# Loading b in 2 MB pairs on SyncE's queue, in a batched 64x64 matmul

## The chip, the cores and the metric

One NeuronCore of one Trainium2 chip runs the whole kernel. The metric is device time in microseconds (us), the median of several executions. The profile is that of one further execution, and its times count from the start of its span.

## The reference

1024 independent products of 64x64 matrices, in fp32:

```python
def setup_inputs():
    return {
        "a": np.random.randn(1024, 64, 64).astype(np.float32),
        "b": np.random.randn(1024, 64, 64).astype(np.float32),
    }

def reference(a, b):
    return np.matmul(a, b).astype(np.float32)
```

Each of `a`, `b` and the output is 16.8 MB in memory, so 33.55 MB are read and 16.78 MB written.

## The kernel before, in words

The batch is cut in 16 tiles `t` of 64 matrices for `b` and the output (1 MB each), and in 8 steps `s` of 128 matrices for `a` (2 MB each); step `s` serves tiles `2s` and `2s+1`.

**a.** `load_a(s)` (L70) brings a step in as four quarters. Three go through GpSimd's queue, which casts them to bf16 on the way (`a_sb`, L74); the fourth goes as fp32 on SyncE's queue (`a_raw`, L78). There are three buffers of each (`A_AHEAD = 3`). Step 0 is special: `load_first_a` brings its four quarters as fp32, two on SyncE's queue and two on ScalarE's (L91). `a` has to be transposed. For steps 1 to 3 (`ON_DVE`) VectorE does that, in `transpose_dve` (L128); its fourth quarter is first cast by ScalarE (L126) out of `a_raw`. For the others `regroup` on VectorE (L109 for the three quarters, L112 for `a_raw`) is followed by transposes on TensorE (L138) and copies out on ScalarE (L141).

**The work of a tile.** `spread(t)` copies the transposed `a` into a block-diagonal tile `at_bd` on VectorE (L154 for tiles 2 to 7, L164 for the others). `cast(t)` makes bf16 out of the fp32 `b_sb` (L173, on VectorE, for tile 0 on ScalarE; the last tile in four parts on both, L178 and L180). `multiply(t)` runs 64 matmuls (L218) and copies the result out of PSUM in eight pieces, mostly on ScalarE (L206). `store(t)` writes a tile out (L195): tiles 0 to 13 on GpSimd's queue, the last two on SyncE's and ScalarE's. Stores are held back by one iteration (`HOLD = 2`).

**b.** `load_b(t)` (L94) loads one tile, 1 MB, in one transfer: even tiles are issued by SyncE, odd ones by ScalarE. `b_pool` has three buffers of 8 KB per partition. So the load of tile `t+3` can be issued when `cast(t)` has read its buffer.

**Queues.** The profile names the three queues by which transfers reach the 16 DMA engines: q0 is GpSimd's (three quarters of `a` from step 1 on, the stores of tiles 0 to 13), q1 is SyncE's (even `b` tiles, `a_raw`), q10 is ScalarE's (odd `b` tiles). Each engine issues its own transfers in program order, among its other instructions.

**Order.** The program is written out by hand (`manual_schedule`). Before the loop: the first `a`, `b` tiles 0 and 1, `load_a(1)`, `load_b(2)`, `load_a(2)`. Iteration `t` of the loop then does `spread(t+1)`, `cast(t+1)`, `load_b(t+3)`, on some even `t` a `load_a`, then `multiply(t)`, the transposing of a later step of `a`, and `store(t-1)`. On SyncE's queue the order is therefore, after the first two quarters of `a`: b0, a_raw 1, b2, a_raw 2, a_raw 3, a_raw 4, b4, a_raw 5, b6, a_raw 6, b8, a_raw 7, b10, b12, b14, stores.

Of the kernel before, what the change touches and what calls it, by code (L numbers as in the profile page):

```python
# [8 lines left out]
fp32 = mybir.dt.float32  # L9
# [4 lines left out]
def kernel(  # L14
# [14 lines left out]
    nc = tc.nc  # L29
# [3 lines left out]

    n_t, n_s = B // 64, B // 128
    A_AHEAD = 3
    B_AHEAD = 3
    N_BD = 2
    HOLD = 2
    ON_DVE = (1, 2, 3)

    a_v = a.rearrange("(s g h) (mp v) k -> s h g mp (v k)", h=4, g=32, v=16)
    b_v = b.rearrange("(t g h) (kp u) n -> t (h kp) g (u n)", h=4, g=16, u=2)
    o_v = out.rearrange("(t gh x) (mo w) n -> t (x mo) gh (w n)", gh=8, x=8, w=4)

    consts = ctx.enter_context(tc.tile_pool(name="consts", bufs=1))
    a_pool = ctx.enter_context(tc.tile_pool(name="a_pool", bufs=A_AHEAD))
    b_pool = ctx.enter_context(tc.tile_pool(name="b_pool", bufs=B_AHEAD))
    work = ctx.enter_context(tc.tile_pool(name="work", bufs=2))
    o_pool = ctx.enter_context(tc.tile_pool(name="o_pool", bufs=8))
    t_psum = ctx.enter_context(  # L50
# [11 lines left out]
    a_tiles, b_tiles, abf_tiles, at_tiles, bbf_tiles = {}, {}, {}, {}, {}  # L62
# [7 lines left out]
    def load_a(s):  # L70

        a_sb = a_pool.tile([128, 3, 16, 64], bf16, name="a_sb")
        for h in range(3):
            nc.gpsimd.dma_start(  # L74
                out=a_sb[:, h, :, :].rearrange("p v k -> p (v k)"), in_=a_v[s, h], single_packet=True
            )
        a_raw = a_pool.tile([128, 16, 64], fp32, name="a_raw")
        nc.sync.dma_start(out=a_raw[:].rearrange("p v k -> p (v k)"), in_=a_v[s, 3])  # L78
        a_tiles[s] = a_sb, a_raw

    def load_first_a():

        raw = [
            o_pool.tile([128, 8, 2, 2, 64], fp32, name="o_sb")[:].rearrange(
                "p gh j wl n -> p (gh j wl n)"
            )
            for _ in range(2)
        ]
        parts = [raw[h % 2][:, 1024 * (h // 2) : 1024 * (h // 2) + 1024] for h in range(4)]
        for h in range(4):  # L90
            (nc.scalar if h % 2 else nc.sync).dma_start(out=parts[h], in_=a_v[0, h])  # L91
        a_tiles[0] = parts

    def load_b(t):  # L94
        b_sb = b_pool.tile([128, 16, 128], fp32, name="b_sb")
        queue = nc.scalar if t % 2 else nc.sync
        queue.dma_start(out=b_sb[:], in_=b_v[t])  # L97
        b_tiles[t] = b_sb

    def regroup(s):  # L100
        a_sb = a_tiles.pop(s)
        a_bf = work.tile([128, 16, 4, 64], bf16, name="a_bf")
        if s == 0:
            for h in range(4):
                copy = nc.scalar.copy if h % 2 else nc.vector.tensor_copy
                copy(a_bf[:, :, h, :], a_sb[h].rearrange("p (v k) -> p v k", v=16))  # L106
        else:
            cast_sb, raw = a_sb
            nc.vector.tensor_copy(  # L109
                a_bf[:, :, 0:3, :], cast_sb[:].rearrange("p h v k -> p v h k")  # L110
            )
            nc.vector.tensor_copy(a_bf[:, :, 3, :], raw[:])  # L112
        abf_tiles[s] = a_bf
        at_tiles[s] = work.tile([128, 32, 4, 4, 4], fp32, name="at_sb")

    def transpose_dve(s, half):
        cast_sb, raw = a_tiles[s]
        if half == 0:
            at_tiles[s] = work.tile([128, 4, 8, 4, 4, 4], fp32, name="at_sb")
        for h in (2 * half, 2 * half + 1):  # L120
            rows = cast_sb[:, h, :, :] if h < 3 else None
            if h == 3:
                rows = work.tile([128, 16, 4, 64], bf16, name="a_bf")[:, 0:4, :, :].rearrange(
                    "p x y k -> p (x y) k"
                )
                nc.scalar.copy(rows, raw[:])  # L126
            pairs = rows.rearrange("p v k -> p (v k)").bitcast(fp32)
            nc.vector.transpose(  # L128
                at_tiles[s][:, h].rearrange("p g w mp vo -> p w vo g mp"),
                pairs.rearrange("p (vo w kp) -> p w vo kp", vo=4, w=4),  # L130
            )

    def transpose(s, j):
        a_cols = abf_tiles[s][:].rearrange("p v h k -> p v (h k)").bitcast(fp32)
        for wl in range(2):
            at_ps = t_psum.tile([128, 4, 128], fp32, name="at_ps")
            for vo in range(4):
                nc.tensor.transpose(  # L138
                    at_ps[:, vo, :], a_cols[:, 4 * vo + 2 * j + wl, :], identity[:]
                )  # L140
            nc.scalar.copy(  # L141
                at_tiles[s][:, :, 2 * j + wl, :, :],
                at_ps[:].rearrange("p vo (g mp) -> p g mp vo", mp=4),
            )

    def spread(t):
        bd = bd_tiles[t % N_BD]
        at_sb = at_tiles[t // 2]
        for h in range(4):
            rows = slice(32 * h, 32 * h + 32)  # L150
            if t // 2 in ON_DVE:
                for i in range(2):
                    block = 32 * (2 * (t % 2) + i)
                    nc.vector.tensor_copy(  # L154
                        bd[rows, 8 * i : 8 * i + 8, :, h, :, :].rearrange(
                            "p g w mp vo -> p (g w) (mp vo)"
                        ),
                        at_sb[block : block + 32, h].rearrange(
                            "p g w mp vo -> p (g w) (mp vo)"
                        ),  # L160
                    )
            else:
                half = slice(16 * (t % 2), 16 * (t % 2) + 16)
                nc.vector.tensor_copy(  # L164
                    bd[rows, :, :, h, :, :].rearrange("p g w mp vo -> p (g w) (mp vo)"),
                    at_sb[rows, half].rearrange("p g w mp vo -> p (g w) (mp vo)"),
                )

    def cast(t):
        b_bf = work.tile([128, 16, 128], bf16, name="b_bf")  # L170
        b_sb = b_tiles.pop(t)
        if t < n_t - 1:
            (nc.vector.tensor_copy if t else nc.scalar.copy)(b_bf[:], b_sb[:])  # L173
        else:
            for gq in range(4):
                rows = slice(4 * gq, 4 * gq + 4)
                if gq % 2:
                    nc.vector.tensor_copy(b_bf[:, rows, :], b_sb[:, rows, :])  # L178
                else:
                    nc.scalar.copy(b_bf[:, rows, :], b_sb[:, rows, :])  # L180
        bbf_tiles[t] = b_bf

    def store(t):
        for piece in held.pop(t):
            piece()
# [53 lines left out]
    with tc.manual_schedule():  # L239
        load_first_a()  # L240

        nc.vector.memset(warm[:, 0:1], 0.0)
        nc.scalar.copy(warm[:, 1:2], warm[:, 0:1])
        load_b(0)
        load_b(1)
        nc.vector.memset(bd_tiles[0][:], 0.0)  # L246
        make_identity(nc, identity)
        nc.gpsimd.memset(bd_tiles[1][:, 0:8], 0.0)
        load_a(1)
        load_b(2)  # L250
        nc.gpsimd.memset(bd_tiles[1][:, 8:16], 0.0)
        load_a(2)
        regroup(0)
        transpose(0, 0)
        transpose(0, 1)
        spread(0)
        cast(0)
        for t in range(n_t):
            s, half = t // 2, t % 2
            if t + 1 < n_t:  # L260
                spread(t + 1)
                cast(t + 1)
            if t + B_AHEAD < n_t:
                load_b(t + B_AHEAD)
            if half == 0 and 0 < s < n_s - 1 - A_AHEAD:
                load_a(s + 1 + A_AHEAD)
            if half == 0 and 0 < s < n_s - 1 and s + 1 not in ON_DVE:
                transpose(s + 1, 1)
            multiply(t)
            if t == 0:  # L270
                transpose_dve(1, 0)
                transpose_dve(1, 1)
                a_tiles.pop(1)
                load_a(A_AHEAD)
                load_a(A_AHEAD + 1)
            if t and s + 2 in ON_DVE and (half or s):
                for part in [0, 1] if t == 1 else [half]:
                    transpose_dve(s + 2, part)
                if half:
                    a_tiles.pop(s + 2)  # L280
            elif half == 0 and 0 < s and s + 2 < n_s:
                regroup(s + 2)
            elif half == 1 and s + 2 < n_s:
                transpose(s + 2, 0)
            if t >= HOLD - 1:
                store(t - HOLD + 1)
        for t in range(n_t - HOLD + 1, n_t):
            store(t)
# [30 lines left out]
```

## Time and profile before

| | us |
|---|---|
| median of three runs | 133.72 (133.57 to 133.80) |
| the profiled execution | 133.61 |
| its span | 131.8 |
| VectorE busy | 101.8 (77% of the span) |
| ScalarE busy | 88.1 (67%) |
| TensorE busy, matmul | 59.6 (45%) |
| GpSimd busy | 31.9 (24%) |
| one `cast` of a b tile on VectorE (L173) | 1.227 |
| from issue to landing of a 1 MB b load, median | 16.5 (14.7 to 22.0) |
| from issue to landing of a 1 MB store on GpSimd's queue, median | 22.7 |
| from issue to landing of an `a_raw` quarter (512 KB), median | 17.3 |

The span is what the instructions of the profiled execution cover; the 1.8 us between it and the time of that execution lie around it. A queue's "share of 16 engines" is the time that its packets took, divided by 16 times the span; as packets overlap a little on an engine, the shares of the queues can sum to slightly over 100%. In a timeline, the bracket behind a line tells how long the engine was idle before it, and what ended that.

### The profile page before, as it was taken

To read this page: it belongs to the slowest core of one execution; us is meant where nothing else is said; L and a number is where in the kernel's file an instruction comes from. 1 tells how busy PE (TensorE), PEld (TensorE's weight loads), DVE (VectorE), ACT (ScalarE), POOL (GpSimd) and SP (SyncE) were. 2 spreads that over 40 slices of the span, in tenths; PEclk is the share of its full clock that TensorE was granted. 3 is DMA by queue.
4 is the path that set the end of the run, shared out by engine and by line. 5 is a ranking of instruction groups with operands and counts; after the bars stand their busy time and mean duration, and the time that the engine had idled before them with its cause. 6 is when DMAs were issued, how large, how long until landed. Compare 5 with 4: busy or idle time off the path is not lost.

```text
span 131.8 us, 2750 instructions
## 1 busy us (share of the span) xinstructions
PE 59.6 (45%) x1104; PEld 56.7 (43%) x1104; DVE 101.8 (77%) x144; ACT 88.1 (67%) x158; POOL 31.9 (24%) x43
## 2 busy tenths in 40 slices
PE   0006405730550640908662883299369619465000
PEld 0006305730550630908552872298368618464000
DVE  5930399529999984999999998699999997898300
ACT  2125414999495096492999989469969996549920
POOL 8991000340054000618031204300420302040000
PEclk9999975798568555595999599558968975579855
DMA  3999999999999999999999999999999999999993
GB/s 68 372 334 313 306 313 280 280 311 321 327 299 400 362 306 297 393 393 400 321 285 357 403 395 362 308 299 385 395 391 393 390 390 397 399 395 406 390 383 136
DMA packets 19020, 44.99 MB, mean 341 GB/s; under 512 B 1088, under 2 KB 3136, under 8 KB 19008
## 3 DMA queue, kind: packets, MB, share of 16 engines
q0 software_dynamic: 6832, 20.19, 50.6%
q1 hardware_dynamic: 7120, 14.68, 30.7%
q10 hardware_dynamic: 5056, 9.96, 20.1%
q8 instruction: 8, 0.13, 0.4%
q14 instruction: 4, 0.03, 0.1%
HBM read 33.55 MB, written 16.78 MB: 382 GB/s over the span
## 4 chain that ended last, share of the span: by engine, by line
DMA 53%; ACT 15%; DVE 14%; PE 6%; issue 5%; SPq 2%; ACTq 0%; DVEq 0%
DMA b_sb<-in_b_dram 53%; ACT o_sb L206 12%; PE o_ps L218 6%; DVE at_bd L164 4%; DVE b_bf L173 4%; DVE at_bd L154 2%; ACT b_bf L173 1%; DVE at_sb L128 1%; DVE o_sb L206 1%; DVE a_bf L109 1%; SPq L91 1%; ACT a_bf L126 1%; SPq L97 1%; ACT b_bf L180 1%; DVE a_bf L112 0%
## 5 line engine op out<-in xcount | busy, mean ns | idle before, releaser
L206 ACT COPY o_sb<-o_ps 64x512 f32<-64x512 f32 x112 | 65.0, 581 | 17.9 <-PE o_ps L218 13.5
L218 PEld LDWEIGHTS <-at_bd 128*128 128x128 bf16 x1024 | 45.2, 117 | 52.6 <-DVE b_bf L173 40.5
L218 PE MATMUL o_ps<-b_bf,at_bd 128*128 128x64 bf16 x960 | 45.6, 223 | 48.7 <-DVE b_bf L173 35.0
L164 DVE COPY at_bd<-at_sb 32x1024 f32<-32x1024 f32 x40 | 29.6, 739 | 6.6 <-ACT at_sb L141 5.6
L195 POOL DMA_DIRECT2D out_dram<-o_sb x14 | 15.4, 1103 | 46.1 <-ACT at_sb L141 20.6
L154 DVE COPY at_bd<-at_sb 32x512 f32<-32x512 f32 x48 | 22.0, 457 | 1.1
L74 POOL DMA_DIRECT2D a_sb<-in_a_dram x21 | 12.4, 606 | 38.5 <-DVE at_sb L128 33.2
L173 DVE CAST b_bf<-b_sb 128x2048 bf16<-128x2048 f32 x14 | 17.2, 1227 | 5.2 <-DMA b_sb<-in_b_dram 4.9
L138 PE MATMUL at_ps<-identity,a_bf 128*128 128x128 f32 x80 | 12.9, 329 | 11.0 <-ACT a_bf L106 11.0
L138 PEld LDWEIGHTS at_ps<-identity,a_bf 128*128 128x128 f32 x80 | 11.7, 176 | 11.0 <-issue 11.0
L141 ACT COPY at_sb<-at_ps 128x512 f32<-128x512 f32 x20 | 10.8, 591 | 2.7 <-PE at_ps L138 2.0
L128 DVE STREAM_TRANSPOSE at_sb<-a_sb 128x512 f32<-128x512 f32 x9 | 8.9, 1065 | 0.0
L128 DVE STREAM_TRANSPOSE at_sb<-a_bf 128x512 f32<-128x512 f32 x3 | 3.1, 1049 | 4.0 <-ACT a_bf L126 4.0
L206 DVE COPY o_sb<-o_ps 64x512 f32<-64x512 f32 x8 | 5.5, 690 | 0.2
L106 ACT CAST a_bf<-o_sb 128x1024 bf16<-128x1024 f32 x2 | 2.1, 1045 | 5.0 <-DMA o_sb<-in_a_dram 5.0
L173 ACT CAST b_bf<-b_sb 128x2048 bf16<-128x2048 f32 x1 | 1.9, 1897 | 4.0 <-DMA b_sb<-in_b_dram 4.0
L126 ACT CAST a_bf<-a_raw 128x1024 bf16<-128x1024 f32 x3 | 3.1, 1046 | 1.7 <-DMA a_raw<-in_a_dram 1.7
L109 DVE COPY a_bf<-a_sb 128x3072 bf16<-128x3072 bf16 x4 | 4.2, 1045 | 0.0
L106 DVE CAST a_bf<-o_sb 128x1024 bf16<-128x1024 f32 x2 | 2.8, 1383 | 1.8 <-DMA o_sb<-in_a_dram 1.8
L246 DVE MEMSET at_bd<- 128x4096 f32 x1 | 3.5, 3472 | 0.8 <-issue 0.8
L206 DVE COPY o_sb<-at_ps 64x256 f32<-64x256 f32 x8 | 3.4, 422 | 0.5 <-PE at_ps L218 0.4
L180 ACT CAST b_bf<-b_sb 128x512 bf16<-128x512 f32 x2 | 1.1, 616 | 3.5 <-DMA b_sb<-in_b_dram 3.5
(16 smaller groups left out, 15.4 us busy)
## 6 DMA issues: line engine op xcount, KB each, us to landing
out_dram<-o_sb POOLq DMA_DIRECT2D x14, 1024.0 KB, 22.7
a_sb<-in_a_dram POOLq DMA_DIRECT2D x21, 256.0 KB, 15.9
a_raw<-in_a_dram SPq DMA_DIRECT2D x7, 512.0 KB, 17.3
o_sb<-in_a_dram SPq DMA_DIRECT2D x2, 512.0 KB, 5.9
o_sb<-in_a_dram ACTq DMA_DIRECT2D x2, 512.0 KB, 7.0
out_dram<-o_sb SPq DMA_DIRECT2D x2, 512.0 KB, 5.5
out_dram<-o_sb SPq DMA_DIRECT2D x2, 256.0 KB, 5.2
out_dram<-o_sb ACTq DMA_DIRECT2D x2, 256.0 KB, 4.7
```

The costliest lines, as they stand in the source:

```text
L74: nc.gpsimd.dma_start(out=a_sb[:, h, :, :].rearrange("p v k -> p (v k)"), in_=a_v[s, h], single_packet=True)
L106: copy(a_bf[:, :, h, :], a_sb[h].rearrange("p (v k) -> p v k", v=16))
L109: nc.vector.tensor_copy(a_bf[:, :, 0:3, :], cast_sb[:].rearrange("p h v k -> p v h k"))
L128: nc.vector.transpose(at_tiles[s][:, h].rearrange("p g w mp vo -> p w vo g mp"), pairs.rearrange("p (vo w kp) -> p w vo kp", vo=4, w=4),)
L138: nc.tensor.transpose(at_ps[:, vo, :], a_cols[:, 4 * vo + 2 * j + wl, :], identity[:])
L141: nc.scalar.copy(at_tiles[s][:, :, 2 * j + wl, :, :], at_ps[:].rearrange("p vo (g mp) -> p g mp vo", mp=4),)
L154: nc.vector.tensor_copy(bd[rows, 8 * i : 8 * i + 8, :, h, :, :].rearrange("p g w mp vo -> p (g w) (mp vo)"), at_sb[block : block + 32, h]. ...
L164: nc.vector.tensor_copy(bd[rows, :, :, h, :, :].rearrange("p g w mp vo -> p (g w) (mp vo)"), at_sb[rows, half].rearrange("p g w mp vo -> p ...
L173: (nc.vector.tensor_copy if t else nc.scalar.copy)(b_bf[:], b_sb[:])
L195: store_queue(t, lo).dma_start(out=o_v[t, :, lo : lo + n, :], in_=o_sb[:, lo : lo + n].rearrange("p gh j wl n -> p (gh j wl n)"),)
L206: copies[2 * par + wl](dst, src)
L218: nc.tensor.matmul(o_ps[:, gl, g % 2, j, :], at_bd[:, j, g, :, u], b_bf[:, g, 64 * u : 64 * u + 64], start=(u == 0), stop=(u == 1),)
```

## The change: b tiles 4 to 13 in pairs

Tiles of `b` are now handled as pairs, pair `p` being tiles `2p` and `2p+1`, in two buffers of 16 KB per partition. Pairs 2 to 6 are loaded by one transfer of 2 MB each, issued by SyncE. Pairs 0, 1 and 7 (`B_ALONE`) are still two transfers of 1 MB, all on SyncE's queue but tile 1. The loads of a pair are issued in the even iterations: pair `s+2` in iteration `t = 2s`, after `cast(t+1)`, which is the last reader of the buffer's former pair `s`. Ahead of the loop, tile 3 is now loaded right behind tile 2, before `load_a(2)`. SyncE's order becomes b0, a_raw 1, b2, b3, a_raw 2, pair 2, a_raw 3, a_raw 4, pair 3, a_raw 5, pair 4, a_raw 6, pair 5, a_raw 7, pair 6, b14, b15, stores. ScalarE issues b1 alone.

```diff
-    B_AHEAD = 3
+    B_ALONE = (0, 1, n_t // 2 - 1)
...
+    b_v2 = b.rearrange("(t g h) (kp u) n -> t (h kp) g (u n)", h=4, g=32, u=2)
...
-    b_pool = ctx.enter_context(tc.tile_pool(name="b_pool", bufs=B_AHEAD))
+    b_pool = ctx.enter_context(tc.tile_pool(name="b_pool", bufs=2))
...
-    def load_b(t):
-        b_sb = b_pool.tile([128, 16, 128], fp32, name="b_sb")
-        queue = nc.scalar if t % 2 else nc.sync
-        queue.dma_start(out=b_sb[:], in_=b_v[t])
-        b_tiles[t] = b_sb
+    def load_b(pair):
+        b_sb = b_pool.tile([128, 2, 16, 128], fp32, name="b_sb")
+        if pair in B_ALONE:
+            for i in range(2):
+                queue = nc.scalar if pair == 0 and i else nc.sync
+                queue.dma_start(out=b_sb[:, i], in_=b_v[2 * pair + i])
+        else:
+            nc.sync.dma_start(out=b_sb[:].rearrange("p i g n -> p (i g) n"), in_=b_v2[pair])
+        for i in range(2):
+            b_tiles[2 * pair + i] = b_sb[:, i]
...
-            (nc.vector.tensor_copy if t else nc.scalar.copy)(b_bf[:], b_sb[:])
+            (nc.vector.tensor_copy if t else nc.scalar.copy)(b_bf[:], b_sb)
...
         load_b(0)
-        load_b(1)
...
         load_a(1)
-        load_b(2)
+        load_b(1)
...
-            if t + B_AHEAD < n_t:
-                load_b(t + B_AHEAD)
+            if half == 0 and s + 2 < n_s:
+                load_b(s + 2)
```

## The prediction, made before the changed kernel ran

> **What bounds the kernel now.** I read the page's slices and queue shares first, then the queues in a short window, then the timelines of VectorE and ScalarE for who waits for a load.
>
> ```profile
> span 131.8 us, 2750 instructions
> DMA  3999999999999999999999999999999999999993
> q0 software_dynamic: 6832, 20.19, 50.6%
> q1 hardware_dynamic: 7120, 14.68, 30.7%
> q10 hardware_dynamic: 5056, 9.96, 20.1%
> ```
>
> The DMA row is full from the first slice to the last, and the shares sum to 101.4%: the 16 DMA engines are the bound, from end to end. The change moves the same bytes. So time can be gained only in the two slices that aren't full (hardly over 0.5 us), but lost wherever DMA comes to stand idle. Next, the queues in 52 to 60 us (packets, MB, share), then in 117.3 to 121 us, when only stores are left:
>
> ```profile
> q0 software_dynamic: 480, 1.70, 58.6%
> q1 hardware_dynamic: 485, 1.00, 33.1%
> q10 hardware_dynamic: 169, 0.35, 11.8%
> ```
>
> ```profile
> q0 software_dynamic: 383, 1.48, 101.9%
> ```
>
> Queues that have work take turns packet by packet (480 against 485); SyncE's and ScalarE's queues each have a turn of their own. Last, the casts on VectorE that wait for a b tile, with the end of VectorE's work, and the one cast of `a_raw` on ScalarE that waits:
>
> ```profile
> 51.23 1.23 DVE L173 CAST b_bf<-b_sb 128x2048 bf16<-128x2048 f32 x1 [2.04 <-DMA b_sb<-in_b_dram]
> ...
> 83.66 1.23 DVE L173 CAST b_bf<-b_sb 128x2048 bf16<-128x2048 f32 x1 [1.63 <-DMA b_sb<-in_b_dram]
> ...
> 112.50 1.23 DVE L173 CAST b_bf<-b_sb 128x2048 bf16<-128x2048 f32 x1 [1.19 <-DMA b_sb<-in_b_dram]
> ...
> 115.19 3.09 DVE L164 COPY at_bd<-at_sb 32x1024 f32<-32x1024 f32 x4
> ```
>
> ```profile
> 35.36 1.05 ACT L126 CAST a_bf<-a_raw 128x1024 bf16<-128x1024 f32 x1 [1.70 <-DMA a_raw<-in_a_dram]
> ```
>
> VectorE waits only 4.9 us for b in all, and is otherwise nearly without a gap: b arrives just in time, and a later b is paid at once.
>
> **Prices.** All are worked out from these rows. A store is 1.05 MB at 403 GB/s: 2.6 us of all 16 engines. A b tile: q10 moves 9.96 MB in 20.1% of 131.8 us, 2.66 us per MB, so 2.8 us; a pair 5.6, an `a_raw` (0.52 MB) 1.4. A quarter of `a` on q0: its 66.7 us less 14 stores, over 21 quarters, 1.4. In packets, by the trace's records: b tile 512 (2 KB each), store 256, `a` quarter and `a_raw` 128 each. One b packet with one q0 packet takes 0.0055 + 0.0102 = 0.0157 us. So against a full q0 a pair on one queue takes 1024 x 0.0157 = **16.0 us**; on two queues, as before, 512 rounds of 0.0212 = **10.8 us**. VectorE needs some 11.7 us for a pair (two casts, 2.46; two spreads, 6.2 to 8; copies or transposes).
>
> **The parts that cost little.** Sixteen b issues become eleven; ScalarE loses seven, with 0.02 us of its own time each and one wait of 0.8 us: 0 to 1 us off an engine 67% busy, hidden behind the casts it waits for; taken as 0. If ScalarE set the end, it would be worth at most that 1 us. No row shows the issue of a 2 MB load: bounded by that of a 1 MB load (0.71 us) and twice that, so up to 0.7 us, five times 3.5 us if nothing covered it; the queue ahead holds 5 us and more of older work each time, so 0. Behind a pair SyncE has only the next `a_raw` and the next pair, and before the change already stood 2 to 11 us on the `a_raw` issues behind a b load (L78) without anyone waiting but the cast shown. The buffers cost nothing: pair s+2 may start after cast(2s+1), exactly when its first tile could before, its second a tile sooner.
>
> The Trainium skill, "DMA: Bandwidth & Descriptors", section "Issuing engines are not separate DMA queues", says that transfers started by several engines interleave on the same 16 DMA engines, and that several issuers save only issuing time. By it the move off ScalarE's queue would cost nothing, and the sum would be 0. The rows above speak for a difference in share; I follow the rows.
>
> **The ledger: order and share on one queue.** Times before are read off the timelines. I take the pure turn-taking and let each wait delay VectorE.
>
> 1. At 22 us a_raw 1 has landed. Before, b2, a_raw 2 followed (32.0, 35.3) with b3 beside them. Now b2, b3, a_raw 2 stand in one line: 1152 packets. Left on q0: seven quarter loads of a and store 0 (issued 28.1), also some 1152. 8 + 8 + 2.7: a_raw 2 at **40.7**, 5.4 later. ScalarE's cast (1.05) ends at 41.8, the last transpose of step 2 (before 37.21 to 38.25) at 42.8: VectorE is 4.6 late. cast(3) runs 47.2 to 48.5.
> 2. Pair 2 starts at 40.7. Against it q0 has three quarter loads of a and stores 1 and 2, 896 packets: 5.6 + 9.1 + a short gap, lands about 55.4. cast(4) would be ready at 53.7 (before 49.2 + 4.5, after which it waited 2.04): it starts at 55.4, **+4.2**.
> 3. a_raw 3 and 4 follow while q0 waits for new work: 56.8 and 58.2. The transposes of step 3 end at 58.9 (before 54.35). All after is 4.5 late; cast(6) is ready at 69.7.
> 4. Pair 3 starts at 58.2; q0 has six quarter loads and stores 3 and 4, 1280 packets, so it is full: 16.0, lands **74.2**. cast(6): before 65.16, now **+9.0**. cast(7) at 79.4.
> 5. a_raw 5 (2.7), pair 4 from 76.9. Now stores come late too, since they wait for tiles: 384 packets at once, 256 at 82.4. 5.6 + 6.5: **89.0**. cast(8) ready at 85.3, starts at 89.0, **+12.8**.
> 6. q0 has run dry. Pair 5, 91.7 to about 100; cast(10) ready at 100.6 (8 + 8 less the wait of 1.63 it had at tile 9): **+11.1**. From here VectorE sets the pace, and DMA idles; cast(14) had waited 1.19, no more: spread(15) ends at 128.2, before 118.28: **+9.9**.
> 7. The tail before: 118.28 to 131.82, the last store 4.6 us behind its issue into full queues. The nearest row for an empty queue is the run's first load, 512 KB in 4.3 us, 1.4 of them moving bytes; 256 KB would so take 3.6. I take 1.0 off (bounds 0 and 2.9, the part of the 4.3 that isn't moving bytes).
>
> Sum: 131.8 + 9.9 - 1.0 = 140.7 of span; + 1.8 around it + 0.1 (the profiled run, 133.61, is 0.11 below the median) = 142.6. Against it: before, transfers on SyncE's queue landed 1 to 2.5 us sooner than pure turn-taking over the real issue times gives, those on q0 3 us later. With each pair 2 us sooner, cast(6) is +7, cast(8) +10.7, and the end 140.5. I take the middle, **141.5 us**.
>
> **Rivals.**
>
> A, *the packets grow*. If a 2 MB load is cut into 4 KB packets, SyncE's queue gets as many bytes a turn as both queues had, and a pair takes 5.6 + 5.2 = 10.8 again. Then pair 2 lands at 51.5 before its cast is ready (53.7, +2.5); pair 3, behind two `a_raw` of 1.4 to 2.7, at 65 to 67.7, before or just as its cast is ready (67.7); the old waits of 1.63 and 1.19 go, and -0.3 is left: DMA stays full, **133.7 us** (133.0 to 135.2), not slower. For it: `a_raw` and the GpSimd stores do go in 4 KB packets. Against it: b's do not, though a partition's 8 KB lies together in SBUF. It decides if the pairs show 512 packets in place of 1024. The chance is 0.13, split nearly evenly over the three outcomes.
>
> B, *q0 runs dry sooner*. Stores and `a` loads wait for the tiles that are late, so SyncE's queue gets the engines alone earlier. If pairs 3 and 4 meet q0 half empty (640 packets each, 12.1 us), pair 3 lands at 70.3, cast(6) is +5.1; pair 4 at about 83.5, after cast(8) is ready (81.4): +7.3; less 1.63 and 1.19 and the tail's 1.0: 3.5, **137.2 us** (135 to 138.5). For it: a_raw 5 to 7 had buffers to spare. Against: in step 4 q0 gets its 1280 packets by 65.5, the times of before plus 4.5, and so in time to be served against pair 3. Chance 0.12.
>
> C, *a 2 MB load leaves gaps*. If its descriptors aren't ready in time, the five pairs lose up to the 3.5 us of issue above, and as much again in the line behind them: 141.5 + 7.0, **148.5 us**, 0.03. For it speaks only that no row shows such a load; against it, that no 1 MB load leaves a gap in the DMA row.
>
> **How the numbers follow.** The forecast, with its own range 138.5 to 146, has 0.72; A 0.13, B 0.12, C 0.03. The predicted time is the forecast's. The range 135 to 146 takes in B and leaves out most of A and C, under 2 in 10; its upper end is the ledger of pure turns with no lead, no saving in the tail and 2 us for issuing. About 0.2% is what a measurement here can tell from no change. Faster: 0.06, most of it from A (and ScalarE's 1 us); same 0.04, from A; slower 0.90.
>
> **What would show it.** In the changed profile: no ScalarE queue traffic in the middle; equal packet counts of q0 and q1 wherever both have work; 1024 packets for a pair; from issue to landing about 16 us and more for the pairs; the ScalarE cast at L126 waiting some 7 us for a_raw 2; VectorE waiting for b at tiles 6 and 8 by 3 to 5 us each; stores landing much sooner than 22.7 us; and digits under 9 in the DMA row in the last third. Wrong would be: a DMA row still full to the end (then A), waits at tiles 4, 6 and 8 under 2 us each (B), or a stretch in which q1 has a pair outstanding and yet DMA isn't busy (C).

## The result, and the profile after

The changed kernel takes **141.57 us** (140.06 to 142.03, four runs) against 133.73 us (133.57 to 133.80): a ratio of 1.057, 95% interval 1.049 to 1.065. Slower, as forecast (141.5 us). The profiled execution is the shortest of its four runs: 140.06 us, with a span of 138.3. So the spans differ by 6.5 us, the medians by 7.8. One run of e9 and one of e11 below fell in a slower state, some 2% above the fastest of their kernel, and the times and ratios leave them out.

Lines of the page after; behind each queue stand packets, MB and the share of 16 engines:

```profile
span 138.3 us, 2729 instructions
DMA  3999999999999999999999999999999999995995
q0 software_dynamic: 6832, 20.19, 48.5%
q1 hardware_dynamic: 10736, 22.02, 46.8%
q10 hardware_dynamic: 1360, 2.62, 5.0%
HBM read 33.55 MB, written 16.78 MB: 364 GB/s over the span
out_dram<-o_sb POOLq DMA_DIRECT2D x14, 1024.0 KB, 11.4
```

The bytes are the same, and the DMA row is still full until the last four slices. A store on GpSimd's queue lands 11.4 us after its issue instead of 22.7: q0 is served sooner. And the engines need longer for the same `b`, fp32 `a` and last stores: q1 and q10 together have 51.8% of 138.3 us, 71.6 us, where before they had 50.8% of 131.8, 67.0 us. That is 4.7 us of the 6.5; q0's own time rose by 0.4 (48.5% of 138.3 against 50.6% of 131.8), and the rest is DMA that stands idle in the last slices (from 124 to 128 us its share is 0.57).

VectorE's and ScalarE's waits for loads, from their timelines (start, length, in brackets the idle time before):

```profile
54.97 1.23 DVE L179 CAST b_bf<-b_sb 128x2048 bf16<-128x2048 f32 x1 [2.41 <-DMA b_sb<-in_b_dram]
...
69.69 1.23 DVE L179 CAST b_bf<-b_sb 128x2048 bf16<-128x2048 f32 x1
...
85.97 1.23 DVE L179 CAST b_bf<-b_sb 128x2048 bf16<-128x2048 f32 x1 [5.46 <-DMA b_sb<-in_b_dram]
...
99.78 1.23 DVE L179 CAST b_bf<-b_sb 128x2048 bf16<-128x2048 f32 x1 [2.30 <-DMA b_sb<-in_b_dram]
```

```profile
40.46 1.04 ACT L132 CAST a_bf<-a_raw 128x1024 bf16<-128x1024 f32 x1 [6.85 <-DMA a_raw<-in_a_dram]
```

These are the casts of tiles 4, 6, 8 and 10, and the cast of a_raw 2. Last, the queues of the changed kernel from 58.8 to 62.2 us, when pair 3 is on its way:

```profile
q1 hardware_dynamic: 480, 0.98, 104.7%
q14 instruction: 1, 0.01, 0.8%
```

q0 isn't in the list: it has nothing to do, though GpSimd issued three loads from 57.49 on:

```profile
57.49 1.65 POOL L75 DMA_DIRECT2D a_sb<-in_a_dram  x3 [9.69 <-DVE at_sb L134]
```

Their first packet starts at 62.40. And q1, alone, fills all 16 engines with 0.98 MB in 3.4 us, some 290 GB/s. A full DMA row can hide a loss: here the engines are busy and slow.

### The profile page after: what moved, and what is told of

Read it like the earlier page. It is cut to its first block, busy times and chain, and to the rows that moved or that the text cites. A ratio compares the mean times of both kernels' runs of the same rounds, so it can differ in the third digit from the quotient of the medians.

```text
span 138.3 us, 2729 instructions
## 1 busy us (share of the span) xinstructions
PE 60.8 (44%) x1104; PEld 57.6 (42%) x1104; DVE 100.6 (73%) x144; ACT 87.8 (64%) x151; POOL 33.0 (24%) x43
## 3 DMA queue, kind: packets, MB, share of 16 engines
q0 software_dynamic: 6832, 20.19, 48.5%
## 4 chain that ended last, share of the span: by engine, by line
DMA 47%; SPq 22%; DVE 15%; ACT 6%; issue 4%; PE 3%; DVEq 0%; ACTq 0%
DMA b_sb<-in_b_dram 28%; DMA a_raw<-in_a_dram 19%; SPq L79 10%; SPq L100 10%; DVE at_bd L170 5%; ACT o_sb L212 5%; DVE b_bf L179 4%; PE o_ps L224 3%; DVE at_bd L160 2%; DVE o_sb L212 2%; SPq L102 1%; SPq L92 1%; DVE at_sb L134 1%; ACT a_bf L132 1%; DVE a_bf L115 1%
## 5 line engine op out<-in xcount | busy, mean ns | idle before, releaser
L224 PE MATMUL o_ps<-b_bf,at_bd 128*128 128x64 bf16 x960 | 47.7, 227 | 57.2 <-DVE b_bf L179 46.5
L224 PEld LDWEIGHTS <-at_bd 128*128 128x128 bf16 x1024 | 47.2, 120 | 61.4 <-DVE b_bf L179 49.6
L201 POOL DMA_DIRECT2D out_dram<-o_sb x14 | 16.8, 1196 | 59.0 <-ACT o_sb L212 27.0
L179 DVE CAST b_bf<-b_sb 128x2048 bf16<-128x2048 f32 x14 | 17.2, 1227 | 10.7 <-DMA b_sb<-in_b_dram 10.3
L160 DVE COPY at_bd<-at_sb 32x512 f32<-32x512 f32 x48 | 20.8, 433 | 1.1
L144 PE MATMUL at_ps<-identity,a_bf 128*128 128x128 f32 x80 | 11.8, 311 | 10.8 <-ACT a_bf L112 10.8
L144 PEld LDWEIGHTS at_ps<-identity,a_bf 128*128 128x128 f32 x80 | 10.7, 164 | 10.8 <-issue 10.8
L118 DVE CAST a_bf<-a_raw 128x1024 bf16<-128x1024 f32 x4 | 3.1, 776 | 0.0
## 6 DMA issues: line engine op xcount, KB each, us to landing
out_dram<-o_sb POOLq DMA_DIRECT2D x14, 1024.0 KB, 11.4
```

Of the source, the lines that this page charges most:

```text
L144: nc.tensor.transpose(at_ps[:, vo, :], a_cols[:, 4 * vo + 2 * j + wl, :], identity[:])
L160: nc.vector.tensor_copy(bd[rows, 8 * i : 8 * i + 8, :, h, :, :].rearrange("p g w mp vo -> p (g w) (mp vo)"), at_sb[block : block + 32, h]. ...
L201: store_queue(t, lo).dma_start(out=o_v[t, :, lo : lo + n, :], in_=o_sb[:, lo : lo + n].rearrange("p gh j wl n -> p (gh j wl n)"),)
L224: nc.tensor.matmul(o_ps[:, gl, g % 2, j, :], at_bd[:, j, g, :, u], b_bf[:, g, 64 * u : 64 * u + 64], start=(u == 0), stop=(u == 1),)
```

## The experiments

Three theories stood against each other. **Theory 1**, turns: the engines serve queues packet by packet, so b on one queue has one turn in two against GpSimd's queue, where two queues had two in three. **Theory 2**, pairing: the 2 MB transfer or the buffers that come free in pairs. **Theory 3**, order: `a_raw` stands behind more of b on SyncE's queue. All times are medians, each taken beside runs of the kernel before on the same chip (133.58 to 133.71 us).

| kernel | us | ratio (95%) |
|---|---|---|
| e3, before, b on SyncE's queue | 138.75 | 1.038 (1.035 to 1.042) |
| e10, the same with four buffers | 139.58 | 1.042 (1.039 to 1.046) |
| e2, pair buffers, 1 MB transfers, SyncE's queue | 140.47 | 1.052 (1.048 to 1.056) |
| e11, the changed kernel again | 141.31 | 1.055 (1.048 to 1.062) |
| e4, pairs on alternate queues | 140.40 | 1.051 (1.048 to 1.054) |
| e5, changed, a_raw on ScalarE's queue | 141.42 | 1.058 (1.053 to 1.062) |
| e6, changed, tile 3 on ScalarE's queue | 141.04 | 1.058 (1.053 to 1.062) |
| e1, pair buffers, two queues, early issue | 144.79 | 1.082 (1.078 to 1.085) |
| **e8, pair buffers, two queues** | **134.79** | **1.007 (1.006 to 1.009)** |
| e9, pairs halved by partitions, two queues | 151.07 | 1.128 (1.123 to 1.133) |

### e1: two queues again, pairs kept

```diff
-        if pair in B_ALONE:
-            for i in range(2):
-                queue = nc.scalar if pair == 0 and i else nc.sync
...
+        for i in range(2):
+            queue = nc.scalar if i else nc.sync
+            queue.dma_start(out=b_sb[:, i], in_=b_v[2 * pair + i])
```

> The changed kernel, its pair buffers and its program order kept, but each pair loaded as two transfers of 1 MB, the odd tile on ScalarE's queue as before the change. Theory 1 (turns: on one queue b gets one turn in two against GpSimd's queue, where two queues got two in three): two turns are back, a pair takes about 11 us against a full GpSimd queue, the waits of 5.5 us at tile 8 and 2.3 us at tile 10 go, 134 us, at most 136. Theory 2 (pairing: two large buffers that come free only in pairs): the buffers are unchanged, so 139 to 142 us. Theory 3 (order: a_raw 2 to 4 stand behind more of b on SyncE's queue): half of b leaves that queue, 134 to 136 us, as theory 1.

It took 144.79 us, the opposite of what theory 1 said. The table of waits tells why (who waits for what: us in all, times, longest), and the page's DMA row where it ends:

```profile
ACT b_sb L99 <- DVE b_bf L176: 25.4, 6, 6.8
```

```profile
DMA  3999999999999999999999999999999993572994
```

ScalarE now issues the odd tile's load in iteration 2s ahead of the copies of multiply(2s), and stands there until cast(2s+1) has freed the pair's buffer: 25.4 us in all, with the PSUM copies queued behind. No cast on VectorE waited for b any more in this run. So it did not test the theories; e8 puts the issue behind those copies.

### e2 and e3: one queue without the 2 MB transfer, and without pairs

```diff
-    B_ALONE = (0, 1, n_t // 2 - 1)
+    B_ALONE = range(n_t // 2)
```

> The changed kernel with every pair as two transfers of 1 MB, both on SyncE's queue. Theory 1: the queue holds the same packets in the same order, 140 to 142 us; the first tile of a pair may land some 5 to 8 us before the second, so tiles 4 and 8 can wait less, at best 139. If the size of the transfer is the cause (2 MB lands only whole, or leaves gaps): 134 to 137 us. Theory 2 (buffers in pairs): 140 to 142 us.

e3 edits the kernel before:

```diff
-        queue = nc.scalar if t % 2 else nc.sync
+        queue = nc.scalar if t == 1 else nc.sync
```

> The kernel before the change (three buffers of 1 MB, single transfers), with all b tiles but tile 1 on SyncE's queue. Theory 1: slower like the changed kernel, 138 to 142 us, with VectorE's waits for b above 8 us and GpSimd's transfers landing in about 11 to 13 us in place of 16 to 23. Theory 2 (pairing) and the size of the transfer: neither is there, 133.5 to 135 us. Theory 3: a_raw 2 is still issued ahead of tile 3, so no early delay of 4 us: 135 to 137 us.

e2 took 140.47 us: 1 MB transfers in place of 2 MB save 1 us or nothing. e3 took 138.75 us without pairs: the one queue alone costs 5.0 us, of 7.8 in the changed kernel. Its VectorE waits 11.8 us for b, where before it waited 4.9, and its `b` and fp32 `a` transfers (q1 and q10) have 51.4% of 136.8, 70.3 us of the engines:

```profile
DVE b_bf L173 <- DMA b_sb<-in_b_dram: 11.8, 5, 4.3
```

```profile
q1 hardware_dynamic: 10816, 22.02, 46.4%
q10 hardware_dynamic: 1360, 2.62, 5.0%
```

Theory 3 alone had 135 to 137 here. Another rival is that SyncE, which now stands longer at its issues, sends b too late. The queues rule it out: in every 4 us from 20 to 120 us q1 moved at least 245 packets in e3 and 211 in the changed kernel, so SyncE's queue never ran empty.

### e4, e5, e6: parts of the traffic back on ScalarE's queue

```diff
-            nc.sync.dma_start(out=b_sb[:].rearrange("p i g n -> p (i g) n"), in_=b_v2[pair])
+            (nc.scalar if pair % 2 else nc.sync).dma_start(out=b_sb[:].rearrange("p i g n -> p (i g) n"), in_=b_v2[pair])
```

> The changed kernel with its 2 MB transfers, pairs 3 and 5 on ScalarE's queue, pairs 2, 4 and 6 on SyncE's. Theory 1: whenever two pairs are in flight at once, or a pair and a_raw, b has two turns in three; since the pairs overlap for only a part of their time, about half of the loss goes: 136 to 139 us. Theory 2 and the size of the transfer: 140 to 142 us. Theory 3: a_raw 5 to 7 no longer stand behind pairs 3 and 5, but a_raw 2 and 3 still do: 138 to 140 us.

140.40 us, outside theory 1's numbers. Part of it is e1's fault again (ScalarE stood 9.8 us at its two pair loads), and tile 8 still waited 6.0 us: a pair on its own still has one turn in two. It decides nothing.

```diff
-        nc.sync.dma_start(out=a_raw[:].rearrange("p v k -> p (v k)"), in_=a_v[s, 3])
+        (nc.scalar if s > 1 else nc.sync).dma_start(out=a_raw[:].rearrange("p v k -> p (v k)"), in_=a_v[s, 3])
```

> The changed kernel with a_raw 2 to 7 issued by ScalarE, so SyncE's queue holds b alone. Theory 1: a_raw takes turns of its own and b is rid of 2.7 us per pair, but a pair alone still takes 16 us against a full GpSimd queue: the early wait for a_raw 2 (6.9 us on ScalarE) goes, the waits at tiles 8 and 10 shrink by some 2 to 3 us: 136 to 139 us. Theory 3 (order alone): all of the loss goes, 133.5 to 135 us.

```diff
-                queue = nc.scalar if pair == 0 and i else nc.sync
+                queue = nc.scalar if pair < 2 and i else nc.sync
```

> The changed kernel with tile 3 alone back on ScalarE's queue (issued ahead of the loop), so that a_raw 2 stands behind tile 2 only. Both theories: ScalarE's wait for a_raw 2 falls from 6.9 us to under 3 and VectorE's wait of 4.2 us at step 2 nearly goes. Theory 1: that is absorbed by longer waits for pairs 2 to 4, since b still has one turn: 139 to 141 us. Theory 3: 4 us of the loss go, 136 to 138 us.

e5 took 141.42 us and e6 141.04: nothing gained, though the early wait did go (ScalarE had no wait for a_raw left in e5, and 1.8 us at a_raw 2 in e6). It came back at the pairs. The casts that waited for b in e5, two in all, from VectorE's timeline:

```profile
58.62 1.23 DVE L179 CAST b_bf<-b_sb 128x2048 bf16<-128x2048 f32 x1 [9.46 <-DMA b_sb<-in_b_dram]
89.19 1.23 DVE L179 CAST b_bf<-b_sb 128x2048 bf16<-128x2048 f32 x1 [5.56 <-DMA b_sb<-in_b_dram]
```

With `a_raw` on a queue of its own, pair 2 has one turn in three while an `a_raw` is on its way (q1 moved 207 packets from 40 to 44 us, beside 113 of q10, and 273 in the next 4 us, with q10 empty), and tile 4 waits 9.5 us instead of 2.4. In both runs ScalarE also stood over 6 us at its last issue ahead of the loop; that made cast(1) 1.7 us late, and by cast(2) it was made up. Theory 3 falls: the order decides where the wait is paid, not how much. Theory 1's 136 to 139 for e5 was also wrong.

### e7: what a b load costs by itself

```diff
...
+        for i in range(n):
+            load(i, nc.sync)
+        gate()
+        for i in range(n):
+            load(i, nc.scalar if i % 2 else nc.sync)
+        gate()
+        for p in range(n // 2):
+            load_pair(p, nc.sync)
+        gate()
...
+        for i in range(n):
+            load(i, nc.sync)
+            store(i)
+        gate()
...
+        for i in range(n):
+            load(i, nc.scalar if i % 2 else nc.sync)
+            store(n + i)
```

> None of the product is computed: 8 MB of b are loaded five times, with a wait for all of it between: as 1 MB transfers on SyncE's queue; as 1 MB transfers on two queues; as 2 MB transfers on SyncE's queue; on SyncE's queue beside 8 MB of stores from GpSimd; on two queues beside 8 MB of stores. The output is zeros but for a few elements. Expected from the changed kernel's trace: one queue alone 116 ns a packet, 8.4 MB in 29 to 30 us (290 GB/s). If a single queue can't keep the DMA engines busy with these packets, two queues take 22 to 25 us; if it is the read of 512 B pieces itself, 29 us again. 2 MB transfers: the same as 1 MB on one queue, 29 to 30 us; with gaps between them 31 or more. Beside stores theory 1 says: packet for packet, so the one queue lands 8 MB in about 40 us or, once the stores are out, a little sooner; the two queues some 8 us sooner.

Stretches out of the middle of the five phases (start and end, length, busy times, then the granted clock, DMA share and GB/s):

```profile
4.00:28.00 24.00, 0.00 (x0) 0.00 (x0) 0.00 (x0) 1.00 1.06 291
36.00:60.00 24.00, 0.00 (x0) 0.68 (x2) 0.00 (x0) 1.00 1.06 291
68.00:92.00 24.00, 0.00 (x0) 0.00 (x0) 0.00 (x0) 1.00 1.06 290
104.00:128.00 24.00, 0.00 (x0) 0.00 (x0) 0.00 (x0) 1.00 1.03 397
152.00:180.00 28.00, 0.00 (x0) 0.34 (x1) 1.46 (x2) 1.00 1.03 393
```

and the queues in the fourth and in the fifth:

```profile
q0 software_dynamic: 1632, 6.29, 67.8%
q1 hardware_dynamic: 1631, 3.24, 35.2%
```

```profile
q0 software_dynamic: 1400, 5.41, 49.9%
q10 hardware_dynamic: 1404, 2.81, 27.3%
q1 hardware_dynamic: 1408, 2.79, 25.9%
```

Two things are measured here. First, the turns: 1632 against 1631 with two queues, 1400, 1404 and 1408 with three. Second, b alone moves 290 GB/s, on one queue or two, in 1 MB or 2 MB: a second queue gains nothing, which was the second of the two cases expected, and 2 MB transfers leave no gaps. Beside stores the same DMA engines move 397 GB/s, with a b packet at 35.2% of 24 us x 16 over 1631, 83 ns, in place of 105.7% of 24 x 16 over 3519, 115 ns. A b load is cheap only while something else is served beside it. So once GpSimd's queue has run dry, everything that is left of b is slow.

### e8 and e9: two queues, ScalarE's issue out of the way

```diff
...
-        if pair in B_ALONE:
-            for i in range(2):
-                queue = nc.scalar if pair == 0 and i else nc.sync
-                queue.dma_start(out=b_sb[:, i], in_=b_v[2 * pair + i])
-        else:
-            nc.sync.dma_start(out=b_sb[:].rearrange("p i g n -> p (i g) n"), in_=b_v2[pair])
+        nc.sync.dma_start(out=b_sb[:, 0], in_=b_v[2 * pair])
...
+    def load_odd(pair):
+        nc.scalar.dma_start(out=b_tiles[2 * pair + 1], in_=b_v[2 * pair + 1])
...
             multiply(t)
+            if half == 0 and s + 2 < n_s:
+                load_odd(s + 2)
...
```

> The pair buffers again with two queues, as two transfers of 1 MB, but ScalarE now issues the odd tile of pair s+2 behind the copies of multiply(2s), so it doesn't stand waiting for cast(2s+1) with those copies behind it, and tile 3 inside the loop. Theory 1 (share of turns): 133.5 to 135.5 us, ScalarE's wait at the b issues under 3 us in all (it was 25.4 in e1), b packets together back to about 67 us of record time. Theory 2 (pair buffers cost by themselves): 138 us or more.

134.79 us: with pair buffers and an early tile 2s+5, though without the 2 MB transfers, only 0.7% is left of 5.7%. The page's queues:

```profile
q0 software_dynamic: 6832, 20.19, 50.3%
q1 hardware_dynamic: 7120, 14.68, 30.5%
q10 hardware_dynamic: 5056, 9.96, 19.9%
```

q1 and q10 have 50.4% of a span of 133.2 us, 67.1 us of the engines, as before the change. ScalarE's waits at its b issues, 4.3 us, were above the 3 expected.

e9, with e8's order of issues, loads partitions 0 to 63 of a pair on SyncE's queue and 64 to 127 on ScalarE's:

```diff
...
-            nc.sync.dma_start(out=b_sb[:].rearrange("p i g n -> p (i g) n"), in_=b_v2[pair])
+            nc.sync.dma_start(
+                out=b_sb[0:64].rearrange("p i g n -> p (i g) n"), in_=b_v2[pair, 0:64]
+            )
...
+            nc.scalar.dma_start(
+                out=b_whole[pair][64:128].rearrange("p i g n -> p (i g) n"),
+                in_=b_v2[pair, 64:128],
+            )
...
```

> As e8, but pairs 2 to 6 are cut by partitions: SyncE loads partitions 0 to 63 of both tiles, ScalarE, behind the copies of multiply(2s), partitions 64 to 127. So a pair lands only whole, as in the changed kernel, but has two turns. Theory 1: 134 to 136 us. If it is the landing in pairs that costs: 138 us or more, with waits for b at even tiles. Each transfer holds half of the partitions; should that keep half of the DMA engines idle, the DMA row would show it and the time says nothing on the theories.

151.07 us, far outside, and not for the reason feared: the DMA row was full to slice 33. Its queues between 48 and 52 us:

```profile
q0 software_dynamic: 323, 1.26, 77.3%
q10 hardware_dynamic: 322, 0.16, 13.7%
q1 hardware_dynamic: 319, 0.16, 13.5%
```

The halves go in packets of 512 B (0.16 MB in 322 packets) in place of 2 KB. The turns are again equal, so both queues together move 1 KB a round beside q0's 4 KB, and pair 2 took over 32 us to land. The small packet itself isn't slow: with q0 empty, from 60.5 to 63.5 us, the halves move at 288 GB/s, as the 2 KB packets do. This wasn't planned, but it is a dose: b's bytes per round of turns were up to 4 KB (before, 133.7 us), 2 KB (changed, 141.6) and 1 KB (e9, 151.1).

### e10 and e11: what is left for the pairs

```diff
-    B_AHEAD = 3
+    B_AHEAD = 4
...
         load_b(2)
+        load_b(3)
```

> The kernel before with all b but tile 1 on SyncE's queue as in e3, and four single buffers in place of three, so that as much of b stands ahead on the queue as with two pairs, a_raw 2 behind tile 3 again. If the 2 us by which e2 is slower than e3 come from b standing deeper on the one queue ahead of a_raw: 140 to 141.5 us, with ScalarE waiting some 7 us for a_raw 2. If they come from buffers that go free in pairs: 138 to 139.3 us as e3.

> The changed kernel once more, beside these on one chip. All theories: 140 to 142.5 us; its second profile tells how far single waits repeat: waits of VectorE for b at tiles 4, 8 and 10 again, tile 8 the longest, 4 to 7 us; b's packets at 71 to 72 us of record time.

With e3's edit as well, e10 took 139.58 us, between its two cases; ScalarE did wait 6.9 us for a_raw 2. So b standing deeper adds about 0.8 us, buffers freed in pairs another 0.9 (e2), and the 2 MB transfer perhaps 1. Only the second of these is clear of noise; the intervals of e3 and e10 overlap, and so do those of e2 and e11. The changed kernel repeated its waits: 2.94, 4.98 and 2.73 us at tiles 4, 8 and 10.

## Why the prediction was right, and where it wasn't

| step | predicted | measured |
|---|---|---|
| 1: a_raw 2 lands; transposes late by | 40.7; 4.6 | 40.4; 4.3 |
| 2: cast(4) starts (before 51.23) | 55.4 | 54.97 |
| 3: a_raw 3 and 4 land | 56.8, 58.2 | 56.8, 58.3 |
| 4: pair 3 lands; cast(6) | 74.2; +9.0 | 68.2; +4.5 |
| 5: pair 4 lands; cast(8) | 89.0; +12.8 | 85.9; +9.7 |
| 6: cast(10); end of spread(15) | +11.1; +9.9 | +10.3; +9.6 |
| 7: tail after spread(15), against 13.5 | 12.5 | 10.4 |
| span | 140.7 | 138.3 |

**The mechanism** held: the share of turns (e3, e8, and as a dose e9), with queue counts equal to a packet or a few in e7. Rival A, that a 2 MB load goes in 4 KB packets, fell: q1's count rose by 3616, about 7 tiles of 512. Rival C, gaps, fell with e7's third phase. The statement of the Trainium skill, "DMA: Bandwidth & Descriptors", section "Issuing engines are not separate DMA queues", that several issuing engines save only issuing time was the wrong guide to this sum: e3 changed only which engine issues the odd tiles of b, and cost 5.0 us.

**Step 4 failed.** It let pair 3 meet "a_raw 3 and 4 follow while q0 waits for new work", and then a full q0 from 58.2 on. In fact q0 had next to nothing (2 packets) from 57.9 to 62.4, since GpSimd's loads, issued at 57.49, began only 4.9 us later. Pair 3 had the engines alone for its first 4 us and landed in 10 us instead of 16, in time for its cast. This is what rival B forecast for that pair, but not for B's reason: the loads weren't issued late (before the change at 53.75, so 3.7 us sooner, where the step reckoned with 4.5), they were slow to start. Pair 4 then met a full q0 and took 15.1 us behind a_raw 5, where the ledger, with q0 thought half empty by then, had 12.1; that gave about half of the error back (the landing was 6.0 us ahead of the ledger at pair 3, 3.1 at pair 4). A wait of 2.30 us at tile 10, which the ledger hadn't, gave back most of the rest.

**Step 6 said "DMA idles".** It doesn't until the last slices: b alone fills the row at 290 GB/s. The prediction's own sign, "a DMA row still full to the end (then A)", would have led a reader wrong. The price of a b packet, 0.0055 us of all engines, was in the main a price beside other traffic; alone a packet takes 115 ns where beside stores it takes 83 (e7). The step's bracket, "8 + 8 less the wait of 1.63", doesn't give +11.1 either; +12.8 of step 5 less 1.63 does.

**Step 7 was mis-sized.** It followed VectorE, but the tail hangs on ScalarE. Before, its last casts waited for b15, and the copies came behind:

```profile
117.28 1.14 ACT L180 CAST b_bf<-b_sb 128x512 bf16<-128x512 f32 x2 [3.55 <-DMA b_sb<-in_b_dram]
```

After, b15 lands at 122.9, just in time, and ScalarE is done with the casts before VectorE has spread tile 15:

```profile
123.25 1.14 ACT L186 CAST b_bf<-b_sb 128x512 bf16<-128x512 f32 x2
```

ScalarE is thus 6.0 us later where VectorE is 9.6, and the span's 6.5 follow ScalarE. The tail saved 3.1 us, past the bound of 2.9. That the forecast still came so close is partly luck: the measured span is 2.4 us under the ledger's, but the profiled run lies 1.5 us under the median, and the forecast had taken 1.1 off the ledger.

**Steps 1 to 3** were right to half a microsecond, but e5 and e6 show that this early delay doesn't add to the end: without it the same time is paid at tiles 4 to 8.

What stays open: the 2 to 3 us between one queue with single buffers (e3) and the changed kernel are spread over three small steps, of which only the middle one (e10 to e2) is clear of noise. No version faster than the kernel before was found. That kernel already moves its 50.3 MB at 382 GB/s over the span, where b beside stores reaches 397.

## What to carry to other kernels

Where DMA is the bound and several queues have work, the number of queues that carry a stream, and the size of its packets, set its share; merging two queues into one takes the stream that the engines downstream wait for from two turns in three to one in two, and lets the other streams run ahead. Look at packet counts by queue in a short window, not at the busy row, and look for stretches in which a stream of small pieces is alone. And a load that an engine issues among its own work must not wait there for a buffer that another engine is still to free (e1: 25 us).

## What the hardware showed that wasn't expected

- Loads made of 512 B pieces reach 290 GB/s alone, on one queue or two and in transfers of 1 MB or 2 MB, and the DMA share reads 1.06 all the while; beside stores the total is 397 GB/s (e7).
- The packets of b follow the shape of the load: 2 KB for 128 partitions, 512 B for 64 (e9).
- GpSimd's loads into an idle queue began 4.9 us after their issue (57.49 to 62.40, changed kernel).
- The DMA that an engine issues behind a b load may hold it: SyncE stood up to 16.2 us on one `a_raw` issue of the changed kernel, and in e1 ScalarE 6.4 us on its second b load before the first cast.
